# A hybrid decoder step in fp32: the input stage, with its sums of squares, warming products, first products and two block loads rearranged

## The chip, the cores and the metric

The kernel runs on one core of a Trainium2 chip. The metric is the device time of one execution in microseconds (us). A core has five engines, each with a queue of its own that it works through in order: PE (matrix products and transposes), ACT and DVE (elementwise work), POOL (elementwise work, masks and memsets) and SP, which here only issues DMAs. They meet through semaphores.

## The reference, cut to what matters

One layer of a decoder: 256 prompt tokens and 8 x 8 sample tokens, 320 in all, with a model width of 2048.

```
h = rms_norm(x, norm_g)                      # x * rsqrt(mean(x*x) + eps) * g
p = einsum('nld,dp->nlp', h, w_in)           # 2048 -> 12416 columns
# branch A (RWKV-7, 16 heads of 64) reads p[:, :4224], branch B (HGRN2, 8 heads of 128) p[:, 4224:8320]
wd, ad = sh[..., 3072:3136], sh[..., 3136:3200]     # sh: token-shifted columns of p
w_log = -softplus(-(w0 + tanh(wd) @ w2)) - 0.5
a = sigmoid(a0 + ad @ a2)
...
merged = sigmoid(p[..., OFF_GA:OFF_GB]) * (y_a @ proj_a) + sigmoid(p[..., OFF_GB:]) * (y_b @ proj_b)
y = x + merged @ w_out                       # then a last rms_norm
```

All of it is float32.

## The kernel before, in words

**Products in three parts.** Each factor of a large product is split into a high part, which PE takes as it is, and the remainder: `hhi` and `hlo` for the activations, `whi` and `wlo` for a weight block of 1024 rows and 128 columns. A tile of 128 columns of `w_in` takes two blocks (`k8` = 0 and 1) of 8 steps, and each step three products: `whi` x `hhi`, `whi` x `hlo`, `wlo` x `hhi`. ACT makes `whi` (a cast), and DVE or POOL makes `wlo` (raw less high). There are three buffers each for the raw block, `whi` and `wlo`.

**The input stage** (lines 354 to 633) makes `hhi` and `hlo` of the 320 tokens. `xts[0]` and `xts[1]` hold 128 prompt tokens each, `xts[2]` the 64 sample tokens. For tile `j`, `squares` sums the squares of each row on ACT (for tile 1 in two halves, which DVE adds), `scale` makes the factor out of the sum (two ACT operations), `gain` multiplies the rows by factor and gain on DVE, `turn(j, k4)` transposes a quarter on PE into PSUM (for tile 2: a half), `high` casts that to `hhi` on ACT, and `low` makes `hlo` on DVE. `warm(n)` issues n products to a PSUM tile `wps` that nobody reads; their operands have 64 rows (`sel` and `gr`). The first tile of `w_in` (columns from 3072, the inputs `wd` and `ad` of the two small lora products) is computed within this stage: `first(k4)` issues its products for steps 4 x `k4` to 4 x `k4` + 3, all three parts. `fetch(b, c0, k8)` loads block `k8` of the columns from `c0` into raw buffer `b`; `divide(b, n, G)` splits that buffer, the difference on POOL, in n pieces. Within the stage the order on PE, ACT, DVE and POOL is that of the code. POOL makes masks and constants ahead of it, and, behind the last difference of a weight block, a long row of memsets for the heads to come (from `jr_all`, line 612).

**The main stream.** `record_all` records the next 68 tiles and the work of 16 and 8 heads, and a planner (`Recorder.order`, with costs and due times of its own) writes out the order for all five engines; all of it carries line 1374. Its tiles follow each other as r, k, v and so on of a pair of heads; block number `ra["n"]` counts up from 0, its raw buffer is `(n + 2) % 3`, and blocks 0 and 1 are loaded and split in the input stage. The lora products (`a<-lora_w`, `a<-lora_a` in the profile) are placed among the main products; for them POOL copies `lora_w` and `lora_a` to the other half of the partitions. Then come the projections and gates (L337 to L339), and the output product (L1454 to L1456).

The numbering of lines is that of the kernel before. In the changed one the lines behind the stage are 17 or 18 higher: 1374 is 1392.

## Time and profile before

| what | value |
|---|---|
| three runs, median | 1170.04 us (1169.23 to 1171.2) |
| the profiled execution, its own time | 1167.92 us |
| its span, first to last instruction | 1166.2 us |
| PE busy | 1140.5 us (98%) |
| DVE, ACT, POOL busy | 779.9, 666.7, 208.9 us |
| granted clock of PE | 0.998 |

A time in the profile counts from the span's start. A row of the timeline or of the chain begins with its start and its duration in us; `x8` is the number of instructions merged into it, and what stands in brackets is the idle time ahead of it and what ended that. The table of stretches gives, for each, its length and then the busy time of PE, PEld (weight loads), DVE, ACT and POOL with the number of instructions, the granted clock of PE, the share of the DMA engines and GB/s. Matmuls overlap: the pitch from start to start, not the duration, says what one more of them costs.

### The profile page before, as it was taken

Reading aid. Unit: us, or ns where it says so; the run is one execution under the profiler, and the core shown is the slowest. Engines: PE = TensorE matmul, PEld = TensorE weight load, DVE = VectorE, ACT = ScalarE, POOL = GpSimd, SP = SyncE. Lnnn points to the kernel's source line nnn. Section 1 sums busy time; section 2 is a strip of 40 time slices with the busy share of each in tenths; the row PEclk is TensorE's granted clock in tenths of the full one; section 3 lists DMA queues with packets and bytes.
Section 4 is the critical chain, followed back from the end, with each engine's and each line's share of the span. In section 5 each row is a group of like instructions: output and inputs, shape, how many; then the busy total and the mean of one; then the engine's idle time right before and its main releaser. Section 6 shows DMA issues by size and latency. Waiting matters only on the chain.

```text
span 1166.2 us, 20745 instructions
## 1 busy us (share of the span) xinstructions
PE 1140.5 (98%) x7791; PEld 1099.2 (94%) x7791; DVE 779.9 (67%) x1625; ACT 666.7 (57%) x1470; POOL 208.9 (18%) x429
## 2 busy tenths in 40 slices
PE   7899999999999999999999999999999999999996
PEld 6899999999999999999999999999999999988865
DVE  6878878878878778778779786444444444444542
ACT  6666766667667667666676667444444444433431
POOL 8532132222322321321421310000000000000000
PEclk9999999999999999999999999999999999999999
DMA  5734535434435435436335435555555555575532
GB/s 168 197 109 114 146 110 129 138 102 124 136 91 150 128 98 145 127 83 164 102 92 166 123 101 137 149 158 146 147 155 151 145 149 157 146 254 162 180 109 90
DMA packets 283833, 159.69 MB, mean 137 GB/s; under 512 B 22990, under 2 KB 273361, under 8 KB 283093
## 3 DMA queue, kind: packets, MB, share of 16 engines
q1 hardware_dynamic: 283220, 154.70, 47.1%
q0 software_dynamic: 512, 3.67, 1.0%
q8 instruction: 61, 1.00, 0.4%
q14 instruction: 40, 0.32, 0.1%
HBM read 148.53 MB, written 9.81 MB: 136 GB/s over the span
## 4 chain that ended last, share of the span: by engine, by line
PE 92%; DVE 3%; DMA 2%; ACT 1%; POOL 1%; issue 1%; DVEq 0%; SPq 0%; ACTq 0%; POOLq 0%
PE mps L1374 40%; PE a L1374 12%; PE mps L338 6%; PE mps L337 6%; PE mps L339 6%; PE b L1374 4%; DMA raw<-in_w_out_dram 2%; PE po L1456 2%; PE po L1454 2%; PE po L1455 2%; PE ppb L338 2%; PE ppa L338 2%; PE ppb L337 2%; PE ppa L337 2%; PE ppb L339 2%; PE ppa L339 2%
## 5 line engine op out<-in xcount | busy, mean ns | idle before, releaser
L1374 PE MATMUL mps<-hlo,whi 128*128 128x320 f32 x1088 | 344.7, 317 | 0.0
L1374 PE MATMUL mps<-hhi,whi 128*128 128x320 f32 x1088 | 344.1, 316 | 0.0
L1374 PE MATMUL mps<-hhi,wlo 128*128 128x320 f32 x1088 | 343.8, 316 | 0.0
L1374 PEld LDWEIGHTS mps<-hlo,whi 128*128 128x128 f32 x1088 | 204.9, 188 | 4.8 <-issue 4.5
L1374 PEld LDWEIGHTS mps<-hhi,whi 128*128 128x128 f32 x1088 | 204.9, 188 | 1.7 <-issue 1.4
L1374 PEld LDWEIGHTS mps<-hhi,wlo 128*128 128x128 f32 x1088 | 204.9, 188 | 0.2
L328 DVE TENSOR_TENSOR wlo<-raw,whi 128x1024 fp32r<-128x1024 f32 x88 | 107.8, 1225 | 125.3 <-ACT whi L327 125.1
L1374 ACT CAST whi<-raw 128x1024 fp32r<-128x1024 f32 x134 | 140.6, 1049 | 80.3 <-PE mps L1374 75.8
L327 ACT CAST whi<-raw 128x1024 fp32r<-128x1024 f32 x88 | 92.2, 1048 | 163.1 <-PE mps L338 104.8
L1374 DVE TENSOR_TENSOR wlo<-raw,whi 128x1024 fp32r<-128x1024 f32 x134 | 168.1, 1255 | 20.0 <-ACT whi L1374 19.4
L337 PE MATMUL mps<-hhi,whi 128*128 128x320 f32 x448 | 138.4, 309 | 0.0
L338 PE MATMUL mps<-hlo,whi 128*128 128x320 f32 x448 | 138.4, 309 | 0.0
L339 PE MATMUL mps<-hhi,wlo 128*128 128x320 f32 x448 | 138.4, 309 | 0.0
L337 PEld LDWEIGHTS mps<-hhi,whi 128*128 128x128 f32 x448 | 84.1, 188 | 0.0
L338 PEld LDWEIGHTS mps<-hlo,whi 128*128 128x128 f32 x448 | 84.1, 188 | 0.0
L339 PEld LDWEIGHTS mps<-hhi,wlo 128*128 128x128 f32 x448 | 84.1, 188 | 0.0
L1447 DVE TENSOR_TENSOR wlo<-raw,whi 128x1024 fp32r<-128x1024 f32 x32 | 39.0, 1224 | 46.4 <-ACT whi L1446 46.1
L1446 ACT CAST whi<-raw 128x1024 fp32r<-128x1024 f32 x32 | 33.6, 1051 | 56.8 <-DMA raw<-in_w_out_dram 26.9
L1429 POOL DMA_DIRECT2D xb<-in_x_sample_dram x1 | 0.7, 721 | 341.2 <-PE mps L339 341.2
L1454 PE MATMUL po<-whi,mhi 128*128 128x512 f32 x128 | 50.4, 393 | 1.7 <-ACT whi L1446 1.0
L1456 PE MATMUL po<-wlo,mhi 128*128 128x512 f32 x128 | 50.5, 394 | 1.3 <-DVE wlo L1447 1.3
L1455 PE MATMUL po<-whi,mlo 128*128 128x512 f32 x128 | 50.1, 391 | 0.0
(408 smaller groups left out, 2341.4 us busy)
## 6 DMA issues: line engine op xcount, KB each, us to landing
raw<-in_w_in_dram SPq DMA_DIRECT2D x194, 512.0 KB
raw<-in_w_out_dram SPq DMA_DIRECT2D x32, 512.0 KB
raw<-in_proj_a_dram SPq DMA_DIRECT2D x16, 512.0 KB
raw<-in_proj_b_dram SPq DMA_DIRECT2D x16, 512.0 KB
s<-in_state_hgrn_dram SPq DMA_DIRECT2D x8, 512.0 KB
out_dram<-s SPq DMA_DIRECT2D x8, 512.0 KB
s<-in_state_rwkv_dram SPq DMA_DIRECT2D x8, 256.0 KB
out_dram<-s SPq DMA_DIRECT2D x8, 256.0 KB
```

The costliest lines, as they stand in the source:

```text
L327: S.copy(hi[:, ks], raw[:, ks])
L328: sub.tensor_sub(lo[:, ks], raw[:, ks], hi[:, ks].bitcast(F32))
L337: T.matmul(dst, hi[:, q, :], xhi[:, k, :], start=(k == 0), stop=False)
L338: T.matmul(dst, hi[:, q, :], xlo[:, k, :], start=False, stop=False)
L339: T.matmul(dst, lo[:, q, :], xhi[:, k, :], start=False, stop=(k == nk - 1))
L1374: o.fn(*o.args, **o.kw)
L1429: G.dma_start(yx[j], src)
L1446: S.copy(hi, raw)
L1447: V.tensor_sub(lo, raw, hi.bitcast(F32))
L1454: T.matmul(pt, h, hi, start=first, stop=False)
L1455: T.matmul(pt, l, hi, start=False, stop=False)
L1456: T.matmul(pt, h, lo, start=False, stop=end)
```

## The change

Five things, all in the input stage but the last.

1. Tile 1's sum of squares is taken in one ACT operation as for the other tiles; the DVE addition goes.
2. `warm` reads a new tile `ones` of 128 rows, which POOL sets to one, instead of `sel` and `gr`. 16 such products stand in front, ahead of the first transposes; then there are 3 and 4, and none around tile 1's transposes.
3. `first(part, k4)` issues one part for four steps. The order is: high x high of steps 0 to 3, of 4 to 7, then the other two parts of steps 0 to 3, and so on. The weight blocks are split in halves by `half` (cast on ACT, difference on POOL), each put between the casts of the tiles.
4. The transposes of tile 1, the gains and the casts move accordingly.
5. Blocks 2 and 3 of the main stream (`k`, columns from 1024) are fetched at the stage's end, and `record_all` begins its own loads with block 4.

```
+        ones = st.tile([128, 256], F32R, name="ones")
+        G.memset(ones.bitcast(F32), 1.0)
 
         def warm(n):
             for _ in range(n):
-                T.matmul(wps[:, :256], sel[:, 0], gr[:, :256], start=True, stop=True)
+                T.matmul(wps[:, :256], ones[:, :128], ones, start=True, stop=True)
...
+            warm(16)
             squares(2)
             scale(2)
             gain(2, 0, 2)
...
             turn(2, 1)
-            warm(3)
+            warm(4)
             squares(0)
             scale(0)
             gain(0, 0, 2)
             turn(0, 0)
             turn(0, 1)
-            warm(4)
+            squares(1)
+            scale(1)
             gain(0, 2, 2)
-            squares(1, 0)
-            squares(1, 1)
-            V.tensor_add(ssq[1][:, 0:1], ssq[1][:, 0:1], ssq[1][:, 1:2])
-            scale(1)
             gain(1, 0)
             turn(1, 0)
-            warm(4)
+            gain(1, 1)
+            turn(1, 1)
...
+            def first(part, k4):
+                w, x = ((whi, hhi), (whi, hlo), (wlo, hhi))[part]
+                for k_ in range(4 * k4, 4 * k4 + 4):
+                    T.matmul(first_ps[:, :NT], w[k4 // 2][:, k_ % 8], x[:, k_], start=part == 0 and k_ == 0,
+                             stop=part == 2 and k_ == KT - 1)
+            def half(b_, hf):
+                ks = slice(4 * hf, 4 * hf + 4)
+                S.copy(whi[b_][:, ks], wraw[b_][:, ks])
+                G.tensor_sub(wlo[b_][:, ks], wraw[b_][:, ks], whi[b_][:, ks].bitcast(F32))
+            half(0, 0)
             high(1, 0)
             low(1, 0)
-            first(0)
+            first(0, 0)
+            gain(1, 2)
+            gain(1, 3)
+            half(0, 1)
             high(2, 1)
             high(0, 1)
             high(1, 1)
...
             turn(0, 2)
+            first(0, 1)
             turn(1, 2)
...
-            first(3)
+            for part in range(3):
+                first(part, 3)
+            fetch(1, 1024, 0)
             divide(0, 1, G)
+            fetch(2, 1024, 1)
...
+                if ra["n"] > 4:
+                    Y.dma_start(raw, win[1024 * k8:1024 * k8 + 1024, c0:c0 + 128].rearrange("(k p) c -> p k c", p=128))
                 if ra["n"] > 2:
-                    Y.dma_start(raw, win[1024 * k8:1024 * k8 + 1024, c0:c0 + 128].rearrange("(k p) c -> p k c", p=128))
                     S.copy(hi, raw)
                     V.tensor_sub(lo, raw, hi.bitcast(F32))
```

What this makes of the queues, at three places. The first is POOL's queue near the end of the masks (`mf` and `mu` are masks, `mk` as well), where the memset of `ones` comes to stand; before:

```order
L452 TENSOR_TENSOR mk<-mk,seqm 128x64 x2
L415 AFFINE_SELECT mf<-mf 64x64
L468 MEMSET mf 64x4x8
L415 AFFINE_SELECT mf<-mf 64x4x8
L468 MEMSET mf 64x2x16
L415 AFFINE_SELECT mf<-mf 64x2x16
L415 AFFINE_SELECT mf<-mf 64x64
L415 AFFINE_SELECT mf<-mf 64x4x8
L415 AFFINE_SELECT mf<-mf 64x2x16
L415 AFFINE_SELECT mf<-mf 64x64
L472 CAST mu_178<-mf 64x192 x2
```

And in the changed kernel:

```order
L468 MEMSET mf 64x2x16
L415 AFFINE_SELECT mf<-mf 64x2x16
L415 AFFINE_SELECT mf<-mf 64x64
L415 AFFINE_SELECT mf<-mf 64x4x8
L517 MEMSET ones 128x256
L415 AFFINE_SELECT mf<-mf 64x64
L415 AFFINE_SELECT mf<-mf 64x2x16
L472 CAST mu_178<-mf 64x192 x2
```

The memset stands behind all that POOL did before, but two selects and the casts to `mu`.

The second place is PE's queue from its first instruction on: `gps` are the products that spread the gain vector, `tps` the transposes (`xt_103` is the 64-token tile, `xt_101` and `xt_102` are tiles 0 and 1), `mps` the first tile's products. Before:

```order
L529 MATMUL gps<-gr,sel 128x512 x4
L503 MATMUL tps<-ident,xt_103 128x64 x8
L519 MATMUL wps<-gr,sel 128x256 x3
L503 MATMUL tps<-ident,xt_103 128x64 x8
L519 MATMUL wps<-gr,sel 128x256 x3
L503 MATMUL tps<-ident,xt_101 128x128 x8
L519 MATMUL wps<-gr,sel 128x256 x4
L503 MATMUL tps<-ident,xt_102 128x128 x4
L519 MATMUL wps<-gr,sel 128x256 x4
L503 MATMUL tps<-ident,xt_102 128x128 x4
L565 MATMUL mps<-hhi,whi 128x320 x4
L565 MATMUL mps<-hlo,whi 128x320 x4
```

And in the changed kernel:

```order
L531 MATMUL gps<-gr,sel 128x512 x4
L521 MATMUL wps<-ones 128x256 x16
L503 MATMUL tps<-ident,xt_103 128x64 x8
L521 MATMUL wps<-ones 128x256 x3
L503 MATMUL tps<-ident,xt_103 128x64 x8
L521 MATMUL wps<-ones 128x256 x4
L503 MATMUL tps<-ident,xt_101 128x128 x8
L503 MATMUL tps<-ident,xt_102 128x128 x8
L564 MATMUL mps<-hhi,whi 128x320 x4
L503 MATMUL tps<-ident,xt_101 128x128 x4
L564 MATMUL mps<-hhi,whi 128x320 x4
L503 MATMUL tps<-ident,xt_102 128x128 x4
```

The 16 products have moved ahead of every transpose, and the first tile's second group of high x high stands ahead of its first remainders.

The third place is ACT's queue from the casts of the transposed tiles on (`hhi` 128x8x64 is tile 2, 128x4x128 a quarter of tile 0 or 1). Before:

```order
L507 CAST hhi<-tps 128x8x64
L507 CAST hhi<-tps 128x4x128
L379 CAST whi<-raw 128x512 x2
L507 CAST hhi<-tps 128x4x128
L507 CAST hhi<-tps 128x8x64
L507 CAST hhi<-tps 128x4x128 x2
L379 CAST whi<-raw 128x512 x2
L507 CAST hhi<-tps 128x4x128 x2
L379 CAST whi<-raw 128x1024
```

And in the changed kernel:

```order
L507 CAST hhi<-tps 128x8x64
L507 CAST hhi<-tps 128x4x128
L570 CAST whi<-raw 128x512
L507 CAST hhi<-tps 128x4x128
L570 CAST whi<-raw 128x512
L507 CAST hhi<-tps 128x8x64
L507 CAST hhi<-tps 128x4x128 x2
L570 CAST whi<-raw 128x512
L507 CAST hhi<-tps 128x4x128 x2
L570 CAST whi<-raw 128x512
L507 CAST hhi<-tps 128x4x128 x2
L379 CAST whi<-raw 128x1024 x2
```

The halves of the weight blocks are spread between the casts of the tiles, and the two whole blocks come last. In the main stream the plan differs in places for the first 300 main products and then no more on PE: the lora products stood behind main products 47 (`lora_w`) and 48 (`lora_a`), and now stand behind 50 (`lora_a`) and 56 (`lora_w`). On SP four block loads stand in a row ahead of the first head's small weights and states, where there were two.

More of the change, by code (lines that the diff above doesn't have):

```diff
@@ L556, in hybrid_step @@
             low(0, 0)
-            pre = [divide(0, 2, G)]
             first_ps = psm.tile([128, 512], F32, name="mps", tag="m")
-            def first(k4):
-                hi, lo = pre[k4 // 2]
-                for w, x, last in ((hi, hhi, False), (hi, hlo, False), (lo, hhi, k4 == 3)):
-                    for k_ in range(4 * k4, 4 * k4 + 4):
-                        T.matmul(first_ps[:, :NT], w[:, k_ % 8], x[:, k_], start=w is hi and x is hhi and k_ == 0,
-                                 stop=last and k_ == KT - 1)
-            gain(1, 1)
-            turn(1, 1)
+            def first(part, k4):
[8 more added lines that the diff above has]
+            half(0, 0)
             high(1, 0)
             low(1, 0)
-            first(0)
+            first(0, 0)
+            gain(1, 2)
+            gain(1, 3)
+            half(0, 1)
             high(2, 1)
@@ L575, in hybrid_step @@
             high(1, 1)
-            gain(1, 2)
             low(2, 1)
@@ L580, in hybrid_step @@
             turn(0, 2)
+            first(0, 1)
             turn(1, 2)
-            pre.append(divide(1, 2, G))
-            gain(1, 3)
-            first(1)
-            for j in range(2):
-                high(j, 2)
-                low(j, 2)
+            first(1, 0)
+            first(2, 0)
+            half(1, 0)
+            high(0, 2)
+            high(1, 2)
+            low(0, 2)
+            low(1, 2)
             turn(0, 3)
             turn(1, 3)
-            divide(2, 1, G)
-            fetch(0, 0, 1)
-            first(2)
-            for j in range(2):
-                high(j, 3)
-                low(j, 3)
+            first(0, 2)
+            first(1, 1)
+            first(2, 1)
+            half(1, 1)
+            fetch(0, 0, 1)
+            high(0, 3)
+            high(1, 3)
+            low(0, 3)
+            low(1, 3)
+            first(1, 2)
+            first(2, 2)
+            divide(2, 1, G)
             ps = pst.tile([128, 512], F32, name="cps", tag="t")
```

## The prediction

> **What bounds the kernel now.** I read the page first (shares, chain), then the busy time in stretches of 10 us, then the chain in order of time and the waits for the first 45 us, where all edits lie.

> ```profile
> span 1166.2 us, 20745 instructions
> PE 92%; DVE 3%; DMA 2%; ACT 1%; POOL 1%; issue 1%; DVEq 0%; SPq 0%; ACTq 0%; POOLq 0%
> ...
> 0.00:10.00 10.00, 2.04 (x4) 1.15 (x4) 4.53 (x6) 5.32 (x7) 8.89 (x37) 1.00 0.73 235
> 10.00:20.00 10.00, 9.56 (x47) 8.22 (x48) 8.23 (x11) 7.61 (x17) 9.53 (x17) 1.00 0.72 200
> 20.00:30.00 10.00, 10.00 (x70) 9.98 (x70) 7.88 (x12) 6.73 (x15) 7.65 (x4) 1.00 0.20 55
> 30.00:40.00 10.00, 6.83 (x48) 6.57 (x46) 7.67 (x15) 5.41 (x12) 9.36 (x37) 1.00 1.01 248
> 40.00:50.00 10.00, 10.00 (x70) 10.00 (x70) 8.76 (x19) 8.18 (x21) 3.17 (x14) 1.00 0.59 168
> ```

> PE (first busy column) carries 92% of the chain and has no gap from 40 us on. It loses time in two places only: nearly all of the first 10 us, and 3.2 us between 30 and 40. What comes later follows PE in step, so the question is how far PE's main stream shifts. POOL (fifth column) is nearly full from the start: every instruction put into its queue there comes late.

> ```profile
> 9.11 1.29 DVE xt L491
> 10.44 1.11 PE tps L503 x8
> 11.56 0.75 PE wps L519 x3
> 12.30 0.85 PE tps L503 x8
> ...
> 18.00 1.15 PE wps L519 x4
> 19.15 1.04 PE tps L503 x4
> 20.19 2.34 PE mps L565 x12
> 22.53 0.87 PE tps L503 x8
> ...
> 29.71 0.31 PE L1374 MATMUL mps<-hhi,whi 128*128 128x320 f32 x1
> PE a L1374 <- POOL lora_w L1374: 3.2, 1, 3.2
> ```

> The rows with `x` are the chain in order of time (start, duration), then one of the timeline and one of the waits. From 10.44, when the first scaled tile is ready, PE goes without a break to its first main product at 29.71. The last row is the later gap: the lora products wait 3.2 us for POOL's copy.

> **The 16 warming products in front.** They read `ones`, and PE takes its matmuls in order, so the first transposes stand behind them and behind the memset. On POOL the memset stands behind three of the five selects on `mf` that begin at 14.69 (POOL's rows of the timeline: start, duration):

> ```profile
> 14.69 1.44 POOL L415 TENSOR_SCALAR_AFFINE_SELECT mf<-mf 64x32 f32<-64x32 f32 x5
> ...
> 15.67 0.45 POOL L415 TENSOR_SCALAR_AFFINE_SELECT mf<-mf 64x32 f32<-64x32 f32 x2
> 16.19 0.72 POOL L472 CAST mu<-mf 64x192 uint8<-64x192 f32 x2
> 33.16 0.32 POOL L624 MEMSET qz<- 128x256 f32 x1
> ```

> The last two of the five start at 15.67, so three are done there, and no row of POOL in this stretch has idle time ahead of it. A memset of that size takes 0.32 (`qz`). So `ones` is ready at 15.67 + 0.32 = 16.0, and PE, ready to transpose at 10.44, stands until then. Everything of the stage is queued behind it: the transposes, ACT's casts of them, and POOL's weight differences, which wait for casts that stand behind those on ACT.

> ```profile
> 19.85 1.41 PE L565 MATMUL mps<-hhi,whi 128*128 128x320 f32 x4
> 20.79 0.47 PE L565 MATMUL mps<-hhi,whi 128*128 128x320 f32 x1
> ...
> 23.83 0.75 PE L565 MATMUL mps<-hlo,whi 128*128 128x320 f32 x4
> ```

> These are PE's rows in narrow stretches of the timeline. Cost of the 16: no row has 256 columns on 128 rows. At the low clock the 320-column product has a pitch of (20.79 - 19.85)/3 = 0.313, by columns 0.25 for 256; the 64-row warming products take at most 1.15/4 = 0.29 each (chain, 18.00). At the high clock, reached between 20.79 and 23.83, 320 columns have (0.75 - 0.31)/3 = 0.147 (the last one lasts 0.31, as at 29.71), so 256 about 0.12. Bounds: 16 x 0.12 = 1.9 and 16 x 0.29 = 4.6. I take 16 x 0.25 = 4.0, since at 16.0 PE has been idle: done at 20.0.

> [...]

> **From there to the main stream.** Of the old 14 warming products, the last two groups (1.15 each) go; 3 and 4 remain between the transposes, now on all rows. I take the high clock from 20.0 on. Sixteen 64-row transposes in two groups at 0.6 each (between 0.85 at the low clock and half of it), 3 and 4 warming products at 0.12, and four transposes of tile 0 at 0.109 (8 in 0.87) make 0.6 + 0.37 + 0.6 + 0.49 + 0.44 = 2.5. So tile 0's first quarter is transposed at 22.5, and leaves the array at 22.7. It was ready for PE long before: DVE's gains need only ACT's sums. The whole sum of squares saves (first row below) one read-out, one ssq addition and ACT's 0.67 wait for it, about 0.8 in all; PE is not there then, so it is worth 0 here (its cover is the wait for `ones`). Without that wait, it would be worth up to 0.8.

> ```profile
> 14.29 0.29 ACT L485 ACTIVATE ssq<-ssq,eps_n 128x1 f32<-128x1 f32 x1 [0.67 <-DVE ssq L548]
> 20.71 1.14 ACT L379 CAST whi<-raw 128x512 fp32r<-128x512 f32 x2
> 23.01 1.07 ACT L507 CAST hhi<-tps 128x512 fp32r<-128x512 f32 x2 [1.15 <-PE tps L503]
> 26.60 1.06 ACT L379 CAST whi<-raw 128x1024 fp32r<-128x1024 f32 x1
> 25.11 2.40 POOL L380 TENSOR_TENSOR wlo<-raw,whi 128x1024 fp32r<-128x1024 f32 x1 [0.70 <-ACT whi L379]
> 27.74 2.40 POOL L380 TENSOR_TENSOR wlo<-raw,whi 128x1024 fp32r<-128x1024 f32 x1 [0.24 <-ACT whi L379]
> ```

> The first tile's products now come part by part, and their second group needs seven casts of ACT in a row from 22.7: five of `hhi` at 0.5 (two in 1.07) and two of half a weight block at 0.57 (two in 1.14), 3.6 in all. PE does first(0,0) and one set of transposes meanwhile and waits, till 26.3. Then PE has the other 11 groups of four products at 4 x 0.147 = 0.587 (6.46), 12 transposes (1.31), the three small ones (0.25), and some 0.15 for `low` of tile 2, which DVE does behind two gains: 8.2. The main stream starts at **34.5 instead of 29.71: +4.8**. The reordering moves no product out of this sum; in before the same products already ran without a gap. Ends for this term: 16 products at the high clock throughout (-2.1) give +2.7; for the other end see the low clock among the rivals.

> **The two block loads and the lora wait.** Blocks 2 and 3 are fetched on SP ahead of the first head's small weights (`w2a`) and states, once POOL has read their buffers for the last time.

> ```profile
> 37.27 1.04 ACT L1374 CAST whi<-raw 128x1024 fp32r<-128x1024 f32 x1 [0.35 <-DMA raw<-in_w_in_dram]
> 28.74 0.48 SPq L1374 DMA_DIRECT2D w2a<-in_rwkv_w_dram  x1
> 39.10 1.05 ACT L1374 CAST whi<-raw 128x1024 fp32r<-128x1024 f32 x1 [0.78 <-DMA raw<-in_w_in_dram]
> ...
> 30.08 0.22 POOL jr_all L612
> 36.72 0.35 POOL L1374 COPY yz<-id 64x128 f32<-64x128 f32 x1
> 37.24 0.30 POOL L1374 COPY yz<-id 64x128 f32<-64x128 f32 x1
> 37.60 0.45 POOL lora_a L1374
> 38.99 0.90 POOL lora_w L1374
> 28.41 2.06 DVE L1374 TENSOR_SCALAR neg<-cols 128x16 f32<-128x16 f32 x1
> ```

> The last rows are POOL's and DVE's, from the chain and the timeline. Before, ACT waits for these two loads (0.35 and 0.78), but PE stands at the lora wait then, so the loads alone gain nothing; they let the plan put lora later, and that they are in time is all I count: 0. The second one waits for POOL's difference of the block that it overwrites, at 33.8 in my sum, and holds `w2a` (28.74 before) back by 5 us, as much as the readers of `w2a` shift: 0 as well. The wait itself is POOL's: from 30.08, the end of its last block difference, its memsets take 38.05 - 30.08 - 0.65 = 7.3 to `lora_a` (two copies go behind it now) and 9.8 to `lora_w`. PE asks for `lora_a` after 50 main products (before: `lora_w` after 47) and for `lora_w` after 56. ACT's last tile casts follow the last transposes, at 29.5 by the sum above; then come one cast (1.06) and two differences of 2.4, each on POOL: its memsets start at 36.2, 1.7 behind the main stream, where before it was 0.4. So `lora_a` comes at 43.5, PE asks at 34.5 + 50 x 0.147 = 41.85: 1.65. `lora_w` comes at 46.0, PE asks at 44.7: 1.3. Together 2.95 instead of 3.2: **-0.25**. Ends: with the old 0.4, the two waits are 0.35 and 1.3 (-1.5); with the two weight differences that DVE now does ahead of lora's own step, and its habit of standing beside POOL (`neg` 2.06, a 16-column operation), 4.5 (+1.3).

> **Sum.** +4.8 - 0.25 = +4.55. The profiled execution took 1167.92 us, 1.72 more than its span, so it would take 1172.5. It lies 2.1 below the median of the runs shown, 1170.04; the forecast for the median is 1170.04 + 4.5 = **1174.5 us**. About 0.2% (2.3 us) is what a measurement of this kernel can tell from no change.

> **Rivals.**
> - The clock stays low. [...] Then PE keeps the old low pitches: 16.0 + 4.6, then 0.85 + 0.75 + 0.85 + 1.15 + 1.04, so the first quarter of tile 0 at 25.2; tile 1's first quarter follows 2 x 1.04 later, leaves the array at 27.5, and five casts from there (2.6) end at 30.1 instead of 26.3: +3.8, in all +8.3, 1178.3. For it: the 0.313 at 20.79. Against: that row's stretch turned high after one microsecond of full-array products, and 16 make more. [...]
> - Not slower: the lora wait goes entirely, -3.2. It decides if POOL starts its memsets 1.3 or more ahead of the main stream instead of 1.7 behind (9.8 to `lora_w`, which PE reaches 8.5 after its start). Time: 4.8 - 3.2 = +1.6, 1171.6. For it: PE comes later. Against: POOL's last two differences wait for casts that stand behind the last transposes, so POOL comes later by as much.
> - The high clock comes early, after five of the first 16, which then take 5 x 0.25 + 11 x 0.12 = 2.6: +3.1, 1173.1. For it: they use all rows without a break. It is the forecast with a smaller term.
> - `ones` is not in PE's way, and the old stage is shortened by the 0.8 of the sums and the lower pitch: 1168 or less. Against: the order of POOL and the full rows up to 16.2.

> **Chances.** Forecast (+3.5 to +6) 0.57; early clock 0.20; low clock 0.11; wait gone 0.08; `ones` no obstacle 0.04. The range runs from the wait gone (1171.5) to the low clock (1178.5). Slower by over 0.2% takes the first three, less a little for an early clock with a shorter wait: 0.87; within 0.2% 0.09; faster 0.04.

> **What would show it.** Right: `ones` on POOL near 15.7, PE's first warming product right behind, tile transposes near 20 instead of 10.44, the first main product between 33 and 36, waits of lora on POOL of 2 to 4 in sum, and the stretches from 60 us on as before but shifted. Wrong: transposes ahead of 15 us (then the memset did not gate), half-clock pitches past 23 us, or a new wait of PE for weights after 45 us, which I have at 0.

## The result: 0.6% slower, and the profile after

The changed kernel takes 1178.33 us (median of six runs, 1173.38 to 1179.41) where the kernel before, run beside it, takes 1169.88 (six runs, 1167.62 to 1171.20). The ratio is 1.0062, with an interval of 1.0048 to 1.0076. A second set of five runs gave 1175.50 and a ratio of 1.0050 [1.0031, 1.0069]. The first six fall into two groups, two at 1173.4 to 1174.1 and four at 1178.2 to 1179.4; of the second five, two lie at 1174.5, one at 1178.83 and two between (1175.50 and 1177.31). The last section compares the two executions that were profiled. Two executions of later variants, 1607 us of the ninth kernel and 1400 us of the eleventh, ran at a mean granted clock of 0.66 and 0.75, and no median below holds them. The profiled execution took 1178.41 us, its span is 1176.7, 10.5 more than before.

First the page of the changed kernel, its span and the chain of work that ended last, by engine; POOL and ACT have a point more of it than before:

```profile
span 1176.7 us, 20763 instructions
...
PE 91%; DMA 2%; DVE 2%; POOL 2%; ACT 2%; issue 1%; DVEq 0%; ACTq 0%; POOLq 0%; SPq 0%
```

The stretches of 10 us (columns as before):

```profile
10.00:20.00 10.00, 3.49 (x16) 3.49 (x16) 5.61 (x6) 4.04 (x8) 7.41 (x16) 1.00 0.73 202
...
40.00:50.00 10.00, 6.21 (x41) 5.68 (x39) 8.29 (x17) 5.58 (x12) 9.48 (x30) 0.98 1.03 252
50.00:60.00 10.00, 9.80 (x49) 9.76 (x49) 4.49 (x14) 5.05 (x14) 2.90 (x12) 0.68 0.20 58
```

From 10 to 20 us PE is busy for 3.49 instead of 9.56, and all of that is the 16 new products. The gap at the lora products is now between 40 and 50. The last row is new: PE is busy nearly all the time, but with 49 matmuls, where a full stretch of the kernel before has 70 to 72, at a granted clock of 0.68.

The timeline, POOL's two rows and then PE's:

```profile
15.16 1.05 POOL L415 TENSOR_SCALAR_AFFINE_SELECT mf<-mf 64x32 f32<-64x32 f32 x3
16.16 0.30 POOL L517 MEMSET ones<- 128x256 f32 x1
...
16.51 3.78 PE L521 MATMUL wps<-ones 128*128 128x256 f32 x16 [10.11 <-POOL ones L517]
20.23 1.11 PE L503 MATMUL tps<-ident,xt 64*128 64x64 f32 x8
...
24.27 2.59 PE L503 MATMUL tps<-ident,xt 128*128 128x128 f32 x16
...
29.08 0.86 PE L564 MATMUL mps<-hhi,whi 128*128 128x320 f32 x4 [0.69 <-ACT hhi L507]
...
37.27 0.31 PE L1392 MATMUL mps<-hhi,whi 128*128 128x320 f32 x1
```

PE stands for 10.11 us at the memset, which itself stands behind POOL's selects. The first transposes begin at 20.23 instead of 10.44, and the main stream at 37.27 instead of 29.71: +7.56.

The lora products, again POOL's rows and then PE's:

```profile
38.85 0.21 POOL L629 MEMSET jr_all<- 128x128 f32 x1
...
46.18 0.67 POOL L1392 CAST lora_a<-lora_a 64x320 fp32r<-64x320 f32 x1
47.02 1.57 POOL L1392 COPY yz<-id 64x128 f32<-64x128 f32 x2
49.70 0.44 POOL L1392 CAST lora_w<-lora_w 64x320 fp32r<-64x320 f32 x1
...
46.91 0.42 PE L1392 MATMUL a<-lora_a,ast 128*128 128x320 f32 x1 [2.14 <-POOL lora_a L1392]
50.20 0.63 PE L1392 MATMUL a<-lora_w,wst 128*128 128x320 f32 x1 [1.85 <-POOL lora_w L1392]
51.16 0.47 PE L1392 MATMUL mps<-hhi,whi 128*128 128x320 f32 x1
51.43 0.47 PE L1392 MATMUL mps<-hlo,whi 128*128 128x320 f32 x1
56.63 0.31 PE L1392 MATMUL mps<-hhi,whi 128*128 128x320 f32 x1
56.77 0.31 PE L1392 MATMUL mps<-hlo,whi 128*128 128x320 f32 x1
```

The two waits are 2.14 + 1.85 = 4.0 instead of 3.2: +0.8. The last four rows show the other new loss: after the second wait the pitch of the main products is 51.43 - 51.16 = 0.27, and later it is 0.14 to 0.15 again. It lasts from 50.20 to about 56.4; half of these 6.2 us is lost, 3.1. Together 7.56 + 0.8 + 3.1 = 11.5. From the 101st main product on (60.29 instead of 48.82) PE runs 11.4 to 11.5 us later, till past 1100 us. The span grew by 10.5, because about 1 us comes back at the output product: the kernel before waits there for `whi` (0.75 and 0.28, from 1117 us on), the changed one doesn't.

### The profile page after: what moved, and what is told of

Same layout as the page of the kernel before. It is cut to its first block, busy times and chain, and to the rows that moved or that the text cites. A ratio compares the mean times of both kernels' runs of the same rounds, so it can differ in the third digit from the quotient of the medians.

```text
span 1176.7 us, 20763 instructions
## 1 busy us (share of the span) xinstructions
PE 1143.9 (97%) x7800; PEld 1102.9 (94%) x7800; DVE 776.1 (66%) x1624; ACT 666.9 (57%) x1468; POOL 212.5 (18%) x430
## 3 DMA queue, kind: packets, MB, share of 16 engines
q0 software_dynamic: 512, 3.67, 0.9%
## 4 chain that ended last, share of the span: by engine, by line
PE 91%; DMA 2%; DVE 2%; POOL 2%; ACT 2%; issue 1%; DVEq 0%; ACTq 0%; POOLq 0%; SPq 0%
PE mps L1392 40%; PE a L1392 12%; PE mps L338 6%; PE mps L337 6%; PE mps L339 6%; PE b L1392 4%; DMA raw<-in_w_out_dram 2%; PE po L1474 2%; PE po L1472 2%; PE po L1473 2%; PE ppb L338 2%; PE ppa L338 2%; PE ppa L337 2%; PE ppb L339 2%; PE ppb L337 2%; PE ppa L339 2%
```

## The experiments

Four theories were in play. A: what costs is the gate, that is, PE waits in order for a memset that stands deep in POOL's queue; move the memset and the loss goes. B: the order of the first tile's products part by part costs by itself. C: the half clock behind the lora products comes from PE's waits there, and goes with them. D: it doesn't come from those waits.

The kernels in one table. "Main" is the start of the first main product in the profiled execution, "lora" the waits of PE at the lora products, "half" the time at a granted clock of 0.50 between 30 and 62 us (windows of 1 us, twice what is missing to 1.00, summed). "Main", "lora" and "half" are of one execution each, the profiled one. The kernel before ran beside each group of them, with medians of 1169.9 to 1170.6. The groups ran on different chips, so a difference of 1 or 2 us between kernels of two groups is weak evidence; 1 to 4, 5 to 8 and 9 to 11 are a group each.

| kernel | median, us | ratio to before | main | lora | half |
|---|---|---|---|---|---|
| before | 1169.88 | 1 | 29.71 | 3.2 | 0 |
| after | 1178.33 | 1.0062 [1.0048, 1.0076] | 37.27 | 4.0 | 6.8 |
| 1 `ones` early | 1167.97 | 0.9978 [0.9963, 0.9992] | 27.00 | 4.2 | 6.8 |
| 2 half array in front | 1168.15 | 0.9982 [0.9967, 0.9996] | 28.18 | 3.9 | 6.8 |
| 3 nothing in front | 1168.65 | 0.9977 [0.9964, 0.9991] | 27.77 | 3.5 | 6.8 |
| 4 before, with front products | 1167.93 | 0.9972 [0.9959, 0.9985] | 27.53 | 3.5 | 6.8 |
| 5 after, differences on DVE | 1172.09 | 1.0014 [0.9999, 1.0029] | 38.19 | 1.8 | 0 |
| 6 `ones` early, differences on DVE | 1164.45 | 0.9948 [0.9933, 0.9963] | 27.93 | 0.7 | 0 |
| 7 `ones` early, loads as before | 1169.38 | 0.9993 [0.9983, 1.0002] | 28.90 | 5.9 | 6.8 |
| 8 after, unaltered | 1175.50 | 1.0050 [1.0031, 1.0069] | 35.32 | 4.1 | 3.4 |
| 9 before, differences on DVE | 1166.65 | 0.9971 [0.9961, 0.9981] | 30.62 | 0 | 0 |
| 10 nothing in front, DVE | 1163.09 | 0.9942 [0.9929, 0.9955] | 28.07 | 0.5 | 0 |
| 11 `ones` early, loads as before, DVE | 1166.17 | 0.9965 [0.9951, 0.9979] | 28.56 | 1.4 | 3.4 |
| 12 no warming at all, DVE | 1162.91 | 0.9935 [0.9915, 0.9954] | 27.50 | 0.7 | 0 |

**1. The memset early.** The changed kernel with the memset put near the head of POOL's queue:

```
         G.memset(rows, 0.0)
+        ones = st.tile([128, 256], F32R, name="ones")
+        G.memset(ones.bitcast(F32), 1.0)
...
-        ones = st.tile([128, 256], F32R, name="ones")
-        G.memset(ones.bitcast(F32), 1.0)
```

> The changed kernel with one edit: the memset of `ones` stands behind the selects on `sel` instead of behind the masks. Theory A (PE stands at the memset): the first warming product starts near 6.5 us, the first transposes near 10.5, no wait of PE on `ones` over 0.5 us, the first main product between 25 and 28 instead of 37.3, and the time falls by 7 to 12 us to 1166 to 1171. Rival B (the order of parts, with seven casts of ACT ahead of the second group of products, makes the stage long): the first main product stays later than 32, and the time falls by less than 4.

Its timeline:

```profile
6.33 3.78 PE L521 MATMUL wps<-ones 128*128 128x256 f32 x16
11.09 0.71 PE L505 MATMUL tps<-ident,xt 64*128 64x64 f32 x8 [0.98 <-DVE xt L493]
...
27.00 0.31 PE L1392 MATMUL mps<-hhi,whi 128*128 128x320 f32 x1
```

The 16 products now run while PE would be idle, and PE waits for DVE's first tile as it did before the change. The main stream begins 10.3 us sooner than in the changed kernel, and the median is 10.4 us lower. This is theory A, on the chip: without the gate, the change loses nothing against the kernel before. A part of the 10.3 is the place at which the high clock comes (experiment 8): against the execution of the changed kernel in which it came early, too, the main stream begins 8.3 us sooner. The half clock after lora stays (6.8 us).

**2 and 3. Half the array in front, and nothing in front.** `warm` on `sel` and `gr` again and no `ones`; the third also without the 16:

```
-        ones = st.tile([128, 256], F32R, name="ones")
-        G.memset(ones.bitcast(F32), 1.0)
...
-                T.matmul(wps[:, :256], ones[:, :128], ones, start=True, stop=True)
+                T.matmul(wps[:, :256], sel[:, 0], gr[:, :256], start=True, stop=True)
...
-            warm(16)      # in the third alone
```

> The changed kernel, but `warm` reads `sel` and `gr` as before (64 rows), so there is no memset to wait for. Theory A: the wait is gone here as well, PE begins to warm near 6.5, time 1167 to 1173. If the full array matters for the clock, the pitch of the products stays at 0.25 or more until the first tile's products, some 1 to 3 us later than in the kernel with `ones` early; if it does not, the two agree within 1 us. Rival B: within 4 us of the changed kernel.

> As the one before, but without the 16 products in front: the rest of the change alone (one sum of squares, order of parts, two loads, 3 and 4 half-array warming products). Theory A: within 2 us of the kernel before, 1167 to 1172, since nothing of the rest costs much. Rival B: 1173 or more, the order of parts being at fault.

The timeline of the third:

```profile
14.10 3.67 PE L503 MATMUL tps<-ident,xt 128*128 128x128 f32 x16
...
27.77 0.31 PE L1389 MATMUL mps<-hhi,whi 128*128 128x320 f32 x1
```

Without any front products the rearranged stage begins its main stream 1.94 us before the kernel before does (27.77 against 29.71), and the median is 0.23% lower. Theory B falls: the order of the parts does not cost. The 16 front products are worth little, on half the rows or on all: 1168.65 without, 1168.15 and 1167.97 with them. The clock rises at different places in these two profiles: in kernel 2 the first eight transposes take 1.11 and the pitches halve only near 18.4 (four products of 320 columns in 1.03 at 18.02, in 0.86 at 20.00), in kernel 1 the first eight transposes, at 11.09, already take 0.71, and the main stream of kernel 2 begins 1.2 us later; the medians don't show it. That the number of rows is the reason is not shown: in kernel 7 the 16 products read all rows, too, and the eight transposes behind them take 1.11.

**4. The kernel before with front products.** The early `ones`, `warm` on it, and `warm(16)` in front, all else as before.

```
+        ones = st.tile([128, 256], F32R, name="ones")
+        G.memset(ones.bitcast(F32), 1.0)
...
-                T.matmul(wps[:, :256], sel[:, 0], gr[:, :256], start=True, stop=True)
+                T.matmul(wps[:, :256], ones[:, :128], ones, start=True, stop=True)
...
+            warm(16)
```

> The kernel before, with `ones` set early, `warm` on the full array and 16 products in front, and nothing else of the change. If early warming is worth something by itself, the clock is high from 14 us or earlier instead of 21, the first main product comes 2 to 4 us earlier than 29.7, and the time is 1166 to 1168 unless the lora wait takes it back; if the stage is held by ACT and DVE instead, the first main product moves by less than 1 us and the time is that of before.

The main stream begins at 27.53 (29.71 before) and the median falls to 1167.93. The waits say why not more; the first row is of this kernel:

```profile
PE tps L505 <- DVE xt L493: 2.4, 3, 1.2
PE a L1377 <- POOL lora_w L1377: 3.5, 1, 3.5
```

With the high clock from 10.5 on (the first eight transposes, at 10.55, take 0.71, where the kernel before has 1.11), PE catches up with DVE's gains and stands there for 2.4 us.

**5 and 6. The last two block differences on DVE.** This takes away what keeps POOL from its memsets, and so the lora waits: once in the changed kernel, once in kernel 1.

```
-            divide(2, 1, G)
+            divide(2, 1, V)
...
-            divide(0, 1, G)
+            divide(0, 1, V)
```

> The changed kernel, with the differences of the two whole weight blocks on DVE (1.2 us each) instead of POOL (2.4 each), so that POOL begins its memsets about 5 us earlier. Theory C (of the loss, some 7 us are the late start of the main stream, and the rest are the two lora waits with the half clock that follows them): the first main product stays near 37, the two waits fall from 4.0 to under 1.5, the clock stays high in 45 to 60 us, and the time falls by 4 to 7 us to 1171 to 1174. Rival D (the half clock after 50 us comes from the input stage or by itself, not from the waits): the clock still falls to 0.5 for some 6 us, and the time falls by less than 3.

> The kernel with `ones` set early, and the same two differences on DVE. Theory C: first main product near 27, lora waits under 1.5 in all, no half clock at 38 to 45 us, time 1161 to 1164. Rival D: half clock as before, time 1164 to 1167.

A wait and the two stretches behind it of kernel 6:

```profile
PE a L1392 <- DVE ast L1392: 0.7, 1, 0.7
...
30.00:40.00 10.00, 8.92 (x60) 8.42 (x60) 7.39 (x15) 6.58 (x16) 5.87 (x20) 1.00 1.13 283
40.00:50.00 10.00, 10.00 (x70) 10.00 (x69) 9.12 (x27) 7.15 (x17) 4.03 (x12) 1.00 0.46 124
```

The granted clock is 1.00 in every stretch of both kernels from 20 us on. Theory C holds, and D falls: with the waits cut from 4.1 and 4.2 to 1.8 and 0.7, the half clock of 3.4 and 6.8 us goes. In its numbers C was a little too bold: kernel 5's wait of 1.8 is over the 1.5 expected, and kernel 6's median of 1164.45 lies above C's range, in D's. The edit is worth 3.5 us in kernel 1 and 6.2 in the changed kernel, or 3.4 against the five runs of the changed kernel that were made beside kernel 5 (8). In kernel 5's profile the main stream began even later than after (38.19), and that execution still took 4 us less. Its ten runs split, too: five at 1169.2 to 1170.6 and five at 1173.6 to 1176.0. The profile, at 1174.46, is one of the upper five and has no half clock after 30 us, so this spread is not that of the lora waits.

**7. The two block loads back with the planner.** Kernel 1 without its two `fetch` lines and with the loads of the main stream from block 2 on, as before.

```
-            fetch(1, 1024, 0)
...
-            fetch(2, 1024, 1)
...
-                if ra["n"] > 4:
-                    Y.dma_start(raw, ...)
                 if ra["n"] > 2:
+                    Y.dma_start(raw, ...)
```

> The kernel with `ones` set early, but the two block loads left to the plan as before, so that lora stands behind main products 47 and 48 again. If the loads and the later place of lora gain as little as the prediction said: within 1 us of the kernel with `ones` early (1167 to 1169), with one lora wait of 3 to 4.5 us instead of two of 2.6 and 1.6. If the loads are worth more, 1170 or more.

```profile
PE a L1389 <- POOL lora_w L1389: 5.9, 1, 5.9
```

The plan then sets lora behind 47 products as in the kernel before, and PE waits 5.9 at once. The median is 1.4 us above kernel 1, between the two ranges expected, and the wait is longer than the 3 to 4.5 expected. The intervals of the two kernels overlap, so that the loads are worth something here, by letting the plan put lora later, is likely and not shown; I had them at nothing. The later main stream (28.90 against 27.00) is not theirs: in this execution the 16 products did not raise the clock, and the first eight transposes take 1.11, as against 0.71 in kernel 1.

**8. The changed kernel once more,** to see its two groups.

> The changed kernel once more, unaltered, for its spread: six runs gave two groups, 1173.4 to 1174.1 and 1178.2 to 1179.4. [...]

```profile
20.37 0.80 PE L503 MATMUL tps<-ident,xt 64*128 64x64 f32 x8
...
35.32 0.31 PE L1392 MATMUL mps<-hhi,whi 128*128 128x320 f32 x1
```

The same program: here eight transposes take 0.80 where they took 1.11, and the main stream begins 1.95 us sooner. The high clock came at 20.62 in this execution, 0.25 after the first transpose had begun, and at 25.66 in the other, 5 us later. And the half clock behind lora lasts 3.4 us here instead of 6.8. The first is worth 1.95 us, the second half of 3.4, together 3.65; the two spans differ by 3.7. So the two terms account for the difference of the two profiles. The five values, though, are 1174.48, 1174.66, 1175.50, 1177.31 and 1178.83, and two of them lie between the groups: if the two effects come and go each by itself, values between are possible, but no execution of that kind was profiled.

**9 to 12. What is worth how much without the lora waits.** The edit of 5 and 6, in the kernel before (9), in kernel 3 (10) and in kernel 7 (11); and kernel 10 without the other seven warming products (12):

```
-            warm(3)
...
-            warm(4)
```

> The kernel before with one edit: the last two block differences of the stage on DVE instead of POOL (none of the change is in it). If the gain of 3.5 us that this edit gave beside the early ones (1164.45 against 1167.97) is that of the lora copies coming in time, it is there without the change as well: lora waits of under 1 us in sum instead of 3.2, no stretch below a granted clock of 0.95 between 35 and 60 us, first main product within 1 us of 29.7, median 1166 to 1167.5 (ratio 0.9965 to 0.998). If it needs the rearranged stage, the median stays within 1 us of the kernel before.

> The changed kernel without the 16 products in front, warming on 64 rows and without ones, as in the run without front products, and the last two differences on DVE. If front products are worth nothing once the lora wait is out of the way: within 0.7 us of the 1164.45 of the early ones with the same edit (1164 to 1165.2). If an earlier high clock is worth its full half of the stage's transposes and products, about 1.5 to 2 us slower than that: 1166 to 1166.5. In both cases lora waits under 1 us and no half clock after 35 us.

> The early ones and the DVE differences, but the two block loads left to the planner as before. If the loads are worth nothing by themselves (the 1.4 us between the two runs with POOL's differences came from the longer lora wait of 5.9 us that followed from the place of lora's products): 1164 to 1165.2, with a lora wait of at most 1.5. If the loads are worth something of their own: 1165.5 to 1166.5, with a wait of ACT for a raw block before 45 us that passes on to PE.

> The run without front products and with DVE's differences (1163.09), now without the other 7 warming products too. Theory: the products on 64 rows and the transposes before 18 us do not raise the clock (there the pitch halves only at 18 to 19, behind the first 128-row products), and PE waits for DVE's gains in that stretch anyway. Then PE has the high clock at the same place, tile transposes at half pitch till 18 to 19, the main stream within 0.5 us of 28.07, and the median within 0.7 us of 1163.09. [...]

The waits of kernel 9, then the timeline of kernel 12:

```profile
PE mps L1374 <- ACT whi L1374: 1.3, 1, 1.3
PE mps L1374 <- DVE wlo L1374: 0.7, 1, 0.7
```

```profile
15.20 1.97 PE L503 MATMUL tps<-ident,xt 128*128 128x128 f32 x8 [0.15 <-DVE xt L491]
...
18.22 0.82 PE L503 MATMUL tps<-ident,xt 128*128 128x128 f32 x4
```

Kernel 9 gains 3.5 us with none of the change in it: no wait for lora is left, and two smaller ones for weights (1.3 + 0.7) come in its place. The two profiled executions differ by 0.8 us only (spans of 1165.4 and 1166.2), and neither has half clock there; that the rest of the 3.5 is half clock in other executions of the kernel before is my estimate from their mean granted clocks (next section); no trace shows it. Kernel 10 against kernel 9 is what the rearranged stage with its loads is worth without front products: 3.6 us. Kernel 11 against kernel 6 puts 1.7 of that on the loads, again with intervals that overlap. Its wait of 1.4 at lora is within what the theory of worthless loads allowed, its median of 1166.17 is not, and it shows the wait that I looked for: 0.7 of PE for `wlo` of a block loaded late. Since 3.4 us at the half clock fell into its profile too, how much of the 1.7 is the loads' own stays open. Kernel 10, at 1163.09, is below both ranges expected and no slower than kernel 6 (the intervals overlap), and kernel 12, with no warming product left, is no slower than kernel 10 (its main stream came 0.57 earlier, 0.5 was the bound expected): in the rearranged stage, warming is worth nothing that can be measured. The clock of kernel 12 rises within the four transposes at 18.22 (0.82, between 1.11 at the low clock and 0.60 at the high one), at 18.68 by the trace's list; in kernel 10 it rises at 19.18 (the four transposes at 19.14 take 0.62). Kernel 12 beats the kernel before by 0.65%, and the changed one by 13 to 15 us (1175.50 and 1178.33).

## Why the prediction was right, and where it was off

The direction and the range held: 1178.33 lies just inside 1171.5 to 1178.5. The likeliest value, 1174.5, was 3.8 too low. That the median came inside, 0.2 from the upper end, is in part luck. The rival of the low clock gave 1178.3, all but the median, but by other terms: it has the main stream at 38.3 (34.5 + 3.8) where it came at 37.27, the lora waits 0.25 shorter where they were 0.8 longer, and nothing for the 3.1 us at the half clock. Of the prediction's own signs, the first main product came later than 33 to 36, and the half-clock pitches lasted to 25.66, past the 23 that it named as wrong. By its steps:

- **The gate.** Foretold at 16.0, measured at 16.46 (16.16 + 0.30). POOL's selects came 0.5 later than in the execution before, and the first product started 0.05 behind the memset. Right.
- **The 16 products.** 4.0 foretold, 20.23 - 16.51 = 3.72 measured, a pitch of 0.23. Right.
- **The clock from 20.0 on.** This is the step that failed. I let the stage run at the high clock from there; in the profiled execution the transposes and warming products behind the 16 still had the old pitches (8 transposes in 1.11, 4 products in 1.22), and ACT's casts of tile 0 began at 25.36 instead of 22.7. The sum had 2.7 for this stretch, measured are 25.36 - 20.23 = 5.1: 2.4 too little. The text had this case as the rival of the low clock, at 25.2, with a chance of 0.11; in kernel 8 the forecast's case came, with the main stream at 35.32 (34.5 foretold). Why it came in one execution and not in the other is not shown. What differs is where the stretches of 3.41 us of the last section lie: in the changed kernel's profile a border of them falls at 18.84, in the midst of the 16 products, in kernel 8's one falls at 17.21 and the next at 20.62. What spoke against the low clock in the prediction, that 16 full-array products are more than the one microsecond of them ahead of the rise in the kernel before (20.19 to 21.37), did not hold: here they ran from 16.51 to 20.23, and the rise came at 25.66.
- **Seven casts, then the rest of PE's work.** 3.6 and 8.2 foretold; 29.08 - 25.36 = 3.7 and 37.27 - 29.08 = 8.19 measured. Right, so the stage is the old sum and 2.77: 0.51 up to the first product, -0.28 of the 16, 2.43 of the clock, 0.12 of the casts.
- **The whole sum of squares.** Nothing, under cover of the wait for `ones`: PE has no other wait than that before 27 us, so it could bring nothing. It was not tried alone; it is part of the 1.9 us that kernel 3 gains in the stage.
- **The lora waits.** 1.65 + 1.3 foretold, 2.14 + 1.85 measured. POOL's memsets began 1.58 behind the main stream (38.85 against 37.27; 1.7 foretold), but took 8.0 to the end of `lora_a` instead of 7.3, and 11.3 to that of `lora_w` instead of 9.8. The second copy of `yz` lies in that: the two took 1.57, where they had taken 0.65. DVE's difference ran beside them:

```profile
47.20 1.23 DVE L1392 TENSOR_TENSOR wlo<-raw,whi 128x1024 fp32r<-128x1024 f32 x1 [0.67 <-ACT whi L1392]
```

The prediction named DVE's differences ahead of lora as the upper end (+1.3) and took -0.25; it became +0.8. The first copy took 0.30. The second begins at 47.37, beside this difference, takes 1.22, and ends at 48.59, 0.16 behind the difference (48.43). In kernels 1 and 2 the second copy is the longer one, too (1.30 and 1.38, after 0.30), in kernel 3 both take 0.30. What holds it up is not shown. The `neg` that the prediction cites for the upper end (2.06, beside a difference on POOL) takes 0.58 in the changed kernel, again beside one, and 0.42 in kernel 6, beside memsets.
- **After the lora waits.** Foretold was no more loss from 45 us on. The 3.1 us lost at the half clock were a term that the sum didn't have: it priced a wait of PE at its length alone.
- **The loads.** Nothing foretold. As foretold, ACT and PE do not wait for them after the change. DVE waits, and the chain runs through the second load (its waits, then the chain):

```profile
DVE dif L1392 <- DMA raw<-in_w_in_dram: 2.0, 1, 2.0
...
36.55 3.70 DMA raw<-in_w_in_dram
```

That costs nothing either, since POOL, on which the lora copies hang, works from 34.12 to past 50 without a gap. But kernels 7 and 11 are 1.4 and 1.7 us above 1 and 6. Neither is clear of its interval; if it holds, "the loads alone gain nothing" was wrong, too: with a plan that sets lora earlier, or a block that comes late, PE waits for it (5.9 in kernel 7, 0.7 in kernel 11).
- **From the profiled execution to the median.** I added 2.1 as if that were a fixed offset. The profiled execution of the kernel before has no half clock ahead of its last 5 us, and its granted clock of 0.998 is rare: of 70 runs of it, the five with a mean granted clock of 0.998 have a median of 1167.8, the 20 with 0.995 have 1170.4, and the 11 with 0.994 have 1171.3. From these clocks I estimate that the median of before holds half clock behind its lora wait too: 0.003 of 1168 us is 3.5 us, which is 7 us at half the clock. That would be why the medians differ by 8.5 and the spans by 10.5; only the one execution has a trace.
- **Where PE loses time before.** The prediction has two places only. There are more, behind 60 us: waits of 5.0 us in sum and the run's last 9 us. But for the 1 us at the output product they are the same in both kernels, so this cost the sum little.

## What to carry to other kernels

Before a warming product is put ahead of real work, look at where its operand is made: a 0.3 us memset behind a full POOL queue held PE for 10.1 us here, and no transpose began before the 16 products had run. Sort out first which waits are left in a stage and whether an idle engine can take the work ahead of them: giving two differences from POOL to DVE (2.40 each on one, 1.21 to 1.25 on the other) was worth 3.2 to 6.2 us in every variant by the medians, more than the 2.2 that front products gained where they gained most (kernel 4). And read the granted clock in stretches just behind a wait, since a wait of PE can cost more than its own length: behind the two waits here, 4.0 us in sum, 3.1 more were lost at the half clock.

## What the runs showed of the hardware

**The clock changes in these traces lie whole multiples of 3.41 us apart.** The time at the half clock in the table is 0, 3.4 or 6.8. The trace's own list of clock changes agrees: in the changed kernel it begins with the rise at 25.66, then comes the fall 23.89 later and the next rise 6.83 behind that, which is 7 and 2 times 3.413. Laid out in such stretches, counted back from the end of the half clock, the changed kernel reads (length, busy PE, and further on the clock):

```profile
18.84:22.25 3.41, 3.41 (x19) 2.85 (x18) 0.26 (x1) 0.58 (x1) 0.00 (x0) 1.00 0.26 79
22.25:25.66 3.41, 3.41 (x20) 3.29 (x20) 0.44 (x1) 0.30 (x1) 0.00 (x0) 1.00 0.00 0
...
42.73:46.14 3.41, 2.04 (x14) 1.77 (x13) 3.00 (x8) 2.74 (x8) 3.28 (x13) 1.00 1.18 292
46.14:49.55 3.41, 1.44 (x8) 1.18 (x8) 2.71 (x5) 1.67 (x4) 3.19 (x7) 1.00 0.98 240
49.55:52.97 3.42, 2.77 (x11) 2.73 (x11) 0.10 (x1) 1.84 (x5) 3.19 (x13) 0.50 0.54 153
52.97:56.38 3.41, 3.41 (x15) 3.41 (x15) 1.68 (x6) 1.10 (x3) 0.10 (x1) 0.50 0.02 5
56.38:59.79 3.41, 3.41 (x25) 3.41 (x24) 2.65 (x7) 2.07 (x7) 0.00 (x0) 1.00 0.05 12
```

And the second execution of the same kernel (kernel 8), then the kernel before, on the grid from its own rise at 21.37:

```profile
17.21:20.62 3.41, 3.41 (x18) 3.19 (x17) 0.00 (x0) 0.00 (x0) 0.55 (x2) 1.00 0.61 176
41.10:44.51 3.41, 1.72 (x12) 1.45 (x10) 3.03 (x7) 2.67 (x7) 3.24 (x14) 1.00 1.18 296
44.51:47.93 3.42, 1.44 (x8) 1.17 (x8) 2.51 (x5) 1.46 (x3) 3.18 (x8) 1.00 0.84 218
47.93:51.34 3.41, 2.98 (x11) 2.94 (x12) 0.00 (x0) 1.96 (x5) 3.14 (x12) 0.50 0.50 146
51.34:54.75 3.41, 3.41 (x25) 3.41 (x25) 2.41 (x7) 2.40 (x6) 0.00 (x0) 1.00 0.03 5
...
35.02:38.44 3.42, 1.74 (x12) 1.48 (x11) 2.14 (x6) 2.00 (x4) 3.21 (x17) 1.00 1.21 293
38.44:41.85 3.41, 1.92 (x13) 1.92 (x14) 2.47 (x3) 2.17 (x5) 3.23 (x10) 1.00 0.71 169
```

One fall in kernel 6 doesn't go by busy time alone. It lies in the stage, ahead of the column "half":

```profile
10.26:13.67 3.41, 2.39 (x23) 2.09 (x23) 3.41 (x4) 3.35 (x5) 3.33 (x3) 1.00 1.13 320
13.67:17.09 3.42, 3.42 (x17) 3.03 (x17) 3.42 (x6) 2.82 (x8) 3.42 (x10) 0.50 0.39 91
```

PE was busy for 2.39 of 3.41 (70%), and the clock fell; in kernel 4 it was busy for 2.24 (66%) from 13.28 to 16.70, and the clock stayed. Of the 2.39, 1.28 are 64-row transposes (11.28 to 11.92 and 12.51 to 13.15), the rest of 1.11 (33%) products; kernel 4's stretch has none of these transposes. Whether that is the reason is not shown.

The same grid reaches back into the stage. In kernel 8 a stretch ends at 20.62, and all but its last 0.25 (17.21 to 20.37) is within the 16 products: the transposes have the high clock from there. In the other execution the borders lie at 18.84, 22.25 and 25.66, no stretch is filled by the 16, and the high clock comes at 25.66 by the grid and by the trace's list (the 16 transposes that begin at 24.27 take 2.59; the same 16 take 1.91 in kernel 8 and 3.67 in kernel 3). The main stream starts 1.95 us apart. That the place of the borders makes the two groups is my estimate from these two profiles; of the changed kernel's other executions no trace was taken. Kernel 5 is a third case: a border at 19.09 lies within its 16 products (16.82 to 20.54), the rise came only at 29.33 (the 16 transposes at 24.58 take 3.62, the four at 29.24 take 0.65), and the main stream started at 38.19. Why no rise came behind the stretch of 18.84 to 22.25, in which PE was busy throughout, and one came behind the next, I can't say: both hold a mixture of full-array products and 64-row transposes.

**In kernel 3 the high clock comes behind transposes on all rows.** The grid has this:

```profile
10.87:14.28 3.41, 3.41 (x23) 3.19 (x23) 3.29 (x4) 3.21 (x9) 3.33 (x4) 1.00 1.17 287
14.28:17.70 3.42, 3.42 (x17) 3.20 (x16) 2.74 (x5) 2.28 (x5) 3.23 (x13) 1.00 0.15 41
```

The first stretch holds 64-row transposes and products, PE is busy throughout, and the pitch stays low (16 transposes of 128 rows in 3.67 from 14.10 on); the second holds 128-row transposes and nearly nothing else, and the high clock is there from 17.70 (four of them in 0.60 at 18.33). In kernels 2 and 11 the clock rises behind a stretch made up mainly of 128-row transposes as well, at 18.43 and 18.73 (in kernel 11 four products of 320 columns take 0.99 at 18.41 and 0.85 at 20.39).

**The granted clock of the views says nothing of the time ahead of the first rise.** In both kernels it reads 1.00 from the start, while the pitches there are twice those behind the rise (in the kernel before 0.313 at 20.79 and 0.147 from 23.83 on): the trace's list of clock changes begins at the first rise (21.37 before, 25.66 after). The falls in it all lie behind that (1161.42 before, 49.55 and 1172.54 after).
